# A recurrent trunk on one core: carried matrix memories in eight buffers instead of five, rotary tables loaded by the attention

## The chip, the core and the metric

The kernel runs on one core of a Trainium2 chip. The core has five engines that work side by side, each on its own list of instructions, in order: TensorE (PE in the profile) multiplies matrices, VectorE (DVE) and ScalarE (ACT) work on elements, GpSimd (POOL) does a few fills here, SyncE (SP) only issues DMAs. An instruction that waits holds up all that stands behind it on its engine. The metric is the device time of one execution in microseconds (us), as the median of several runs.

## What is computed

Two layers. Each normalises its input (512 prompt tokens and 8 samples of 16 tokens, 640 in all, 1024 wide), projects it with one large matrix, and feeds three mixers: a gated linear recurrence (RG-LRU), a matrix-memory recurrence (mLSTM, 4 heads of 256) and a sliding-window attention with rotary positions. Their outputs are projected, gated, added and projected again; an MLP with 4096 hidden channels follows. The part that matters here is the mLSTM's step with a carried memory C, which each of the 8 samples brings along for each head as a 256 x 256 matrix:

```python
def mlstm_chunk(carry, inp):
    C, n, m = carry
    q, k, v, ig, lf = inp
    ...
    num = jnp.einsum('bhts,bhsd->bhtd', w, v) + inter_w[..., None] * jnp.einsum('bhtd,bhde->bhte', q, C)
    ...
    C_new = decay[..., None, None] * C + jnp.einsum('bhs,bhsd,bhse->bhde', wk, k, v)
    n_new = decay[..., None] * n + jnp.einsum('bhs,bhsd->bhd', wk, k)
```

C is read, used against the queries of the 16 tokens, decayed, updated, and written out. In the attention, queries and keys are turned by cosines and sines of their positions (`rope`).

## The kernel before

All matmuls keep fp32 accuracy by splitting operands into a high and a low part (`split`, and for weights lines 164 and 166: ACT casts `wraw` to `whi`, DVE subtracts to get `wlo`), so that a product takes three matmuls. Weights stream from HBM through SP's queue (`wraw`, L212 and L155). The order of the instructions on each engine isn't written out by hand: a scheduler walks a simulated timeline when the kernel is built and takes on each engine what is ready, so work of different stages interleaves. Tiles come from pools; `bufs` is the number of buffers behind one name, and a new tile in a used buffer waits until all earlier work on that buffer is done.

`mlstm` runs over 4 heads. In each head four projections of the head's columns go through PE (L327): keys `ktok` (evicted by ACT), queries `qT` (DVE, L642), values `vt` (ACT, L649) and an output gate `mo`. The prompt's recurrence over chunks comes next, and in its last chunk `sample` (L577 to L624) handles the 8 samples. For each sample b:

- a buffer `cb` of 128 x 2 x 258 is taken (L600, five buffers), SP loads the sample's 256 KB matrix into it (L601), and DVE copies the two columns of the normaliser beside it (L602);
- ACT casts `cb` to `ch` (L605) and DVE makes the rest `cl` (L606), two buffers each;
- PE multiplies the queries `qm` with `ch` and `cl` (L609, four matmuls), and the stored rows `kvs` with one another (L613, two);
- DVE decays `cb` and adds the second product (L615, two instructions), SP stores `cb` to `out_C_s` (L617), and ACT takes the normaliser column (L618, `nsr`).

The rows in `kvs` go out to DRAM and come back in another layout (`sdr`, stores L585 and L586, loads L593), also on SP. Per layer that is 32 loads and 32 stores of 256 KB. The head ends with `num` (L731), scaled by DVE and transposed by PE (L737). The last lines of `mlstm` (L743 to L752) write the normalisers through a tile `nrt`.

The rotary tables `cos2` and `sin2` are columns 392 to 1031 of a constant tile `cs`, loaded at the start (L446) and kept in SBUF throughout. In each layer's `attention`, DVE multiplies them with a row of weights (L759 and L760). The sample part of it loads `vc` (L910), the old values of the window, and copies it (L912).

Of the kernel before, what the change touches and what calls it, by code (L numbers as in the profile page):

```python
# [9 lines left out]
F32 = mybir.dt.float32  # L10
# [45 lines left out]
NCST = 128 * 3 + 8 + 640  # L56
# [19 lines left out]
def trunk(ctx: ExitStack, tc: tile.TileContext, I, O):  # L76
    nc = tc.nc
    depth = I["w_in"].shape[0]
    cst = I["const"]
    pe, act, dve, pool, sp = nc.tensor, nc.scalar, nc.vector, nc.gpsimd, nc.sync  # L80

    const = ctx.enter_context(tc.tile_pool(name="const", bufs=1))
# [4 lines left out]
    psB = ctx.enter_context(tc.tile_pool(name="psB", bufs=4, space=PSUM))  # L87
    dram = ctx.enter_context(tc.tile_pool(name="scr", bufs=1, space=bass.MemoryType.DRAM))

    cs = const.tile([128, NCST], F32, name="cs")  # L90
    sp.dma_start(cs[:, 0:128], cst[:, 0:128])
    ident = cs[:, 0:128]
    maskp = cs[:, 128:256]
    masks = cs[:, 256:384]
    bmask = cs[:, 384:392]
    cos2 = cs[:, 392:712].rearrange("p (t d) -> p t d", d=64)
    sin2 = cs[:, 712:1032].rearrange("p (t d) -> p t d", d=64)
    ones = const.tile([128, 128], F32, name="ones")
    pool.memset(ones, 1.0)

# [8 lines left out]
    def ps_small():  # L109
        return psB.tile([128, 512], F32, name="psb", tag="psb")  # L110
# [16 lines left out]
    def split(dst, src, scale=None):  # L127

        if scale is None:
            act.copy(dst[:, 0], src)  # L130
            dve.tensor_tensor(dst[:, 1], src, dst[:, 0].bitcast(F32), ALU.subtract)
        else:
            act.activation(dst[:, 0], src, AF.Copy, scale=scale)  # L133
            dve.scalar_tensor_tensor(dst[:, 1], src, scale, dst[:, 0].bitcast(F32), op0=ALU.mult, op1=ALU.subtract)

    def act_tile(p=None):
        return (p or actp).tile([128, 2, NT], F32R, name="at", tag="at")
# [290 lines left out]
    with tc.tile_pool(name="ld", bufs=1) as ld:  # L428
        xin = ld.tile([128, 5, D], F32, name="xin")
        xss = ld.tile([128, 10], F32, name="xss")  # L430
        xpr = I["x_prompt"][0].rearrange("(t p) d -> p t d", p=128)

        def load(h):
            c = slice(512 * h, 512 * h + 512)
            sp.dma_start(xin[:, 0:2, c], xpr[:, 0:2, c])
            sp.dma_start(xin[:, 2:4, c], xpr[:, 2:4, c])
            sp.dma_start(xin[:, 4, c], I["x_sample"].rearrange("b s d -> (b s) d")[:, c])

        load(0)
        for _ in prep(0, 0):  # L440
            pass
        load(1)
        for _ in prep(0, 1):
            pass
        prepared[0] = 1
        sp.dma_start(cs[:, 128:NCST], cst[:, 128:NCST])  # L446
        xs, u = [], []
        for m in range(8):
            x = xp.tile([128, NT], F32, name="x", tag="x")
            ps = ps_small()  # L450
            for t in range(4):
                pe.transpose(ps[:, 128 * t:128 * t + 128], xin[:, t, 128 * m:128 * m + 128], ident)
            dve.tensor_copy(x[:, 0:512], ps)
            ps = ps_small()
            pe.transpose(ps[:, 0:128], xin[:, 4, 128 * m:128 * m + 128], ident)
            act.copy(x[:, 512:640], ps[:, 0:128])
            xs.append(x)
            u.append(act_tile())
            split(u[m], x, cv[:, 8 * V_N1 + m:8 * V_N1 + m + 1])
            if m % 4 == 1:  # L460
                h = m // 4
                for t in range(5):
                    xsq = ld.tile([128, 512], F32, name="xsq", tag="xsq", bufs=2)
                    act.activation(xsq, xin[:, t, 512 * h:512 * h + 512], AF.Square, accum_out=xss[:, 5 * h + t:5 * h + t + 1])
        dve.tensor_tensor(vv[:, 0:5], xss[:, 0:5], xss[:, 5:10], ALU.add)
# [86 lines left out]
    def mlstm(l, gp, gpp, mp, half, hdp):  # L552
# [24 lines left out]
        def sample(h, kw, vt, pn, out):  # L577


            st = mp.tile([128, 1028], F32R, name="st", tag="st", bufs=1)  # L580
            for o, n, src in ((0, 256, kw), (512, 258, vt[:, 4, :])):
                act.copy(st[:, o:o + n], src)
                dve.tensor_tensor(st[:, o + n:o + 2 * n], src, st[:, o:o + n].bitcast(F32), ALU.subtract)
            for i, (a, b) in enumerate(((0, 512), (0, 770), (256, 512))):
                sp.dma_start(sdr[h][:, i, 0:256], st[:, a:a + 256].bitcast(F32))  # L585
                sp.dma_start(sdr[h][:, i, 256:514], st[:, b:b + 258].bitcast(F32))  # L586

            def rows(g):

                kv = kvs[g % 2]  # L590
                sd = sdr[h][32 * g:32 * g + 32].rearrange("(b s) i d -> s i b d", s=16)
                for i in range(3):
                    sp.dma_start(kv[16 * i:16 * i + 16].bitcast(F32), sd[:, i])  # L593
                return kv

            pg = [ps_small(), ps_small()]
            for b in range(DB):
                if b % 2 == 0:
                    kv = rows(b // 2)
                cb = mp.tile([128, 2, 258], F32, name="cb", tag="cb", bufs=5)  # L600
                sp.dma_start(cb[:, :, 0:256], I["state_mlstm_C"][l, b, h].rearrange("(k p) e -> p k e", p=128))  # L601
                dve.tensor_copy(cb[:, :, 256:258], nT[:, :, 8 * b + 2 * h:8 * b + 2 * h + 2])  # L602
                ch = mp.tile([128, 2, 258], F32R, name="ch", tag="ch", bufs=2)
                cl = mp.tile([128, 2, 258], F32R, name="cl", tag="cl", bufs=2)
                act.copy(ch, cb)  # L605
                dve.tensor_tensor(cl, cb, ch.bitcast(F32), ALU.subtract)  # L606
                for kt in range(2):
                    for c in (ch, cl):
                        pe.matmul(pg[b // 4][:, 0:258], qm[:, kt, 128 * b:128 * b + 128], c[:, kt, :],  # L609
                                  start=(b % 4 == 0 and kt == 0 and c is ch), stop=(b % 4 == 3 and kt == 1 and c is cl))  # L610
                for kt in range(2):
                    ps = ps_small()
                    pe.matmul(ps[:, 0:258], kv[:, b % 2, 128 * kt:128 * kt + 128], kv[:, b % 2, 256:514],  # L613
                              start=True, stop=True)
                    dve.scalar_tensor_tensor(cb[:, kt, :], cb[:, kt, :], decb[:, h, 4 + b:5 + b], ps[:, 0:258],  # L615
                                             op0=ALU.mult, op1=ALU.add)
                sp.dma_start(O["C_s"][l, b, h].rearrange("(k p) e -> p k e", p=128), cb[:, :, 0:256])  # L617
                act.copy(nsr[:, b, h, :], cb[:, :, 256])  # L618
                if b % 4 == 3:

                    g = b // 4
                    here, there = slice(64 * g, 64 * g + 64), slice(64 - 64 * g, 128 - 64 * g)
                    act.copy(out[here], pg[g][there, 0:258])
                    dve.tensor_tensor(out[here], out[here], pg[g][here, 0:258], ALU.add)  # L624

        for h in range(4):
# [45 lines left out]
            for kt in range(2):  # L672
                dve.tensor_tensor(qs[:, kt, :], qT[:, kt, 128:512], iw[:, 0:384], ALU.mult)
                dve.tensor_tensor(qw[:, kt, :], qT[:, kt, 512:640], iw[:, 384:512], ALU.mult)
                d = qm[:, kt, :].rearrange("p (b t) -> p b t", t=144)
# [9 lines left out]
            for t in range(5):  # L685
# [30 lines left out]
                sq = mp.tile([128, 256], F32, name="sq", tag="sq", bufs=1)  # L716
# [15 lines left out]
            for e in range(2):  # L732
# [7 lines left out]
                pe.transpose(ps[:, 0:128], num[:, 4, 128 * e:128 * e + 128], ident)  # L740
                act.activation(yt[:, 512:640], ps[:, 0:128], AF.Copy, scale=half(V_MG, k))
                act.dma_start(ydr[0][128 * k:128 * k + 128, :], yt)
        nrt = mp.tile([8, 128], F32, name="nrt", tag="nrt")  # L743
        ps = ps_small()
        pe.transpose(ps[0:8, 0:128], npr, ident)
        dve.tensor_copy(nrt[0:8, :], ps[0:8, 0:128])
        sp.dma_start(O["n_p"][l, 0].rearrange("h (k p) -> (h k) p", p=128), nrt[0:8, :])
        nrs = mp.tile([64, 128], F32, name="nrs", tag="nrt")
        ps = ps_small()
        pe.transpose(ps[0:64, 0:128], nsr.rearrange("p b h k -> p (b h k)"), ident)  # L750
        dve.tensor_copy(nrs, ps[0:64, 0:128])
# [1 line left out]


    def attention(l, ap):
        def tables(o):
            tabs = ap.tile([128, 2, 5, 64], F32, name="tabs", tag="tabs")
            gq = rowb[:, o:o + 64].unsqueeze(1).to_broadcast([128, 5, 64])
            dve.tensor_tensor(tabs[:, 0], cos2, gq, ALU.mult)  # L759
            dve.tensor_tensor(tabs[:, 1], sin2, gq, ALU.mult)  # L760
            return tabs
# [37 lines left out]
        gemm_x(u, ev_kv)  # L799
        kd = ap.tile([128, 5, 2, 2, 64], F32, name="kd", tag="q", bufs=2)  # L800
        norm_rope(ksb[:, :, 0:128].rearrange("p t (h d) -> p t h d", d=64), 2, tables(64), kd[:, :, :, 0, :])
        act.copy(kd[:, :, :, 1, :], kd[:, :, :, 0, :])
        for nm, t_ in (("k", kd), ("v", vd)):
# [18 lines left out]
        qsm = ap.tile([128, 8, 8, 16], F32, name="qsm")  # L822
        pool.memset(qsm, 0.0)
        qtabs = tables(0)


# [173 lines left out]
    for l in range(depth):  # L1000
# [224 lines left out]
        with tc.tile_pool(name="at", bufs=1, reuse_waits="tile") as ap:  # L1225
            attention(l, ap)
# [18 lines left out]
        with tc.tile_pool(name="ml", bufs=1, reuse_waits="tile") as mp:  # L1245
            mlstm(l, gp, gpp, mp, half, hdp)
# [255 lines left out]
```

## Time and profile before

| | |
|---|---|
| median of 3 runs | 2889.65 us (2889.05, 2889.65, 2895.65) |
| profiled execution | 2888.68 us, its span 2886.9 us |
| PE busy | 2834.2 us, 98% |
| DVE busy | 1842.2 us, 64% |
| ACT busy | 1306.7 us, 45% |
| granted TensorE clock | 0.998 |

A busy share of 98% means that PE has 52.7 us of the span in which it stands still. The profile names for each such stretch the last event that released the engine. The mLSTM stages lie at about 480 to 840 us (layer 0) and 1930 to 2270 us (layer 1).

### The profile page before, as it was taken

The numbers are of one execution on the slowest core, as the hardware profiler recorded it, in microseconds if no ns is written. First come the engines' busy times: TensorE is split into PE (matmuls) and PEld (weight loads), VectorE is DVE, ScalarE is ACT, GpSimd is POOL, SyncE is SP. The second block draws the span as 40 slices with busy tenths as digits, with TensorE's granted clock in tenths as the row PEclk, the third lists the DMA queues.
The fourth block names the chain that finished last, engine by engine and source line by source line (L and its number), as shares of the span: only waits on it lengthen the run. The fifth ranks groups of instructions, "written<-read, shape, count | busy, mean of one in ns | idle before, by whom it ended". The sixth has DMA issues, their size and how long they took to land. (4 is left out here: it accounts for less than half of the span.)

```text
span 2886.9 us, 50824 instructions
## 1 busy us (share of the span) xinstructions
PE 2834.2 (98%) x20158; PEld 2794.1 (97%) x20158; DVE 1842.2 (64%) x3746; ACT 1306.7 (45%) x2761; POOL 26.7 (1%) x65
## 2 busy tenths in 40 slices
PE   8999999999999999999999999999999999999999
PEld 8999999999999999999999999999999999999999
DVE  7967576444554677676779676655455646767772
ACT  5764444333432444445357544443444424443452
POOL 0000000000000000000000000000000000000000
PEclk9999999999999999999999999999999999999999
DMA  5242224344474322222322322334444733222222
GB/s 174 65 124 81 71 86 124 117 134 143 150 259 132 110 75 87 81 74 87 113 61 79 117 72 86 94 101 142 127 142 148 268 121 103 74 88 74 81 81 81
DMA packets 276878, 319.53 MB, mean 111 GB/s; under 512 B 26424, under 2 KB 231016, under 8 KB 276608
## 3 DMA queue, kind: packets, MB, share of 16 engines
q1 hardware_dynamic: 267104, 300.03, 33.9%
q10 hardware_dynamic: 9536, 16.26, 1.6%
q8 instruction: 158, 2.59, 0.4%
q14 instruction: 80, 0.66, 0.1%
HBM read 255.76 MB, written 62.04 MB: 110 GB/s over the span
## 5 line engine op out<-in xcount | busy, mean ns | idle before, releaser
L309 PE MATMUL acc<-at,whi 128*128 128x320 f32 x5120 | 818.1, 312 | 6.8 <-ACT at L133 2.8
L309 PEld LDWEIGHTS acc<-at,whi 128*128 128x128 f32 x5120 | 765.3, 189 | 10.1 <-ACT at L133 3.5
L164 ACT CAST whi<-wraw 128x512 fp32r<-128x512 f32 x682 | 407.8, 619 | 489.0 <-PE acc L309 181.9
L166 DVE TENSOR_TENSOR wlo<-wraw,whi 128x512 fp32r<-128x512 f32 x682 | 451.4, 691 | 169.6 <-ACT whi L164 107.4
L327 PE MATMUL acc<-whi,at 128*128 128x256 f32 (+1 forms) x3040 | 408.3, 284 | 16.5 <-DVE qT L642 4.3
L309 PE MATMUL acc<-at,wlo 128*128 128x320 f32 x2560 | 415.0, 310 | 0.0
L327 PEld LDWEIGHTS acc<-whi,at 128*128 128x128 f32 x3040 | 377.9, 188 | 21.8 <-DVE qT L642 5.6
L309 PEld LDWEIGHTS acc<-at,wlo 128*128 128x128 f32 x2560 | 383.7, 188 | 0.7
L255 PE MATMUL acc<-at,whi 128*128 128x320 f32 x1440 | 245.0, 311 | 2.1 <-DVE ha L1375 0.6
L255 PEld LDWEIGHTS acc<-at,whi 128*128 128x128 f32 x1440 | 217.5, 188 | 8.3 <-ACT whi L164 4.7
L327 PE MATMUL acc<-wlo,at 128*128 128x256 f32 (+1 forms) x1520 | 218.0, 282 | 0.0
L327 PEld LDWEIGHTS acc<-wlo,at 128*128 128x128 f32 x1520 | 196.1, 188 | 0.2
L293 PE MATMUL psb<-at,whi 128*128 128x320 f32 x896 | 170.6, 309 | 0.0
L293 PE MATMUL acc<-at,whi 128*128 128x320 f32 x896 | 169.0, 309 | 0.0
L293 PEld LDWEIGHTS psb<-at,whi 128*128 128x128 f32 x896 | 141.3, 188 | 0.0
L293 PEld LDWEIGHTS acc<-at,whi 128*128 128x128 f32 x896 | 140.9, 188 | 0.0
L255 PE MATMUL acc<-at,wlo 128*128 128x320 f32 x720 | 133.5, 308 | 0.0
L164 ACT CAST whi<-wsum 128x512 fp32r<-128x512 f32 x120 | 74.2, 620 | 130.1 <-PE acc L293 100.1
L255 PEld LDWEIGHTS acc<-at,wlo 128*128 128x128 f32 x720 | 112.5, 188 | 0.0
L166 DVE TENSOR_TENSOR wlo<-wsum,whi 128x512 fp32r<-128x512 f32 x120 | 82.4, 687 | 44.8 <-ACT whi L164 39.1
L293 PE MATMUL acc<-at,wlo 128*128 128x320 f32 x448 | 101.7, 308 | 0.0
L293 PE MATMUL psb<-at,wlo 128*128 128x320 f32 x448 | 100.5, 308 | 0.0
(378 smaller groups left out, 3651.4 us busy)
## 6 DMA issues: line engine op xcount, KB each, us to landing
wraw<-in_w_in SPq DMA_DIRECT2D x160, 512.0 KB
wraw<-in_w_up SPq DMA_DIRECT2D x64, 512.0 KB
wraw<-in_w_down SPq DMA_DIRECT2D x64, 512.0 KB
cb<-in_state_mlstm_C SPq DMA_DIRECT2D x64, 256.0 KB
out_C_s<-cb SPq DMA_DIRECT2D x64, 256.0 KB
gdr<-sg ACTq DMA_DIRECT2D x32, 320.0 KB
rl<-ydr SPq DMA_DIRECT2D x32, 320.0 KB
sg<-gdr SPq DMA_DIRECT2D x32, 320.0 KB
```

The lines of the kernel that those rows point to most:

```text
L164: act.copy(hi if shape else hi[:, :, :src.shape[-1]], src)
L166: dve.tensor_tensor(lo if shape else lo[:, :, :src.shape[-1]], src, h.bitcast(F32), ALU.subtract)
L255: pe.matmul(bank[nm], ws[i][:, k, :], xs(nm, k)[:, part], start=(first and i == 0 and k == 0 and part == 0), stop=(i == 1 and k == 3), ski ...
L293: pe.matmul(o[s], lhs, hs[k][:, part, 320 * s:320 * s + 320], start=(k == 0 and i == 0 and part == 0), stop=(i == 1 and k == 3))
L309: pe.matmul(acc[:, s, 0:320], lhs, xs[k][:, part, 320 * s:320 * s + 320], start=(i == 0 and k == 0 and part == 0), stop=(i == 1 and k == 7),)
L327: pe.matmul(o, xs[k][:, part, 128 * t:128 * t + 128], wt[:, k % KQ, 0:n], start=(i == 0 and k == 0 and part == 0), stop=(i == 1 and k == 7),)
```

## The change

The tile `cs` shrinks from 1032 to 392 columns, which frees 2560 bytes in each partition; its load at the start shrinks with it. The rotary tables get a tile `trig` in the pool of each layer's attention, with a DMA of 320 KB of their own, once per layer. The buffers of `cb` go from five to eight, and the two tiles `nrt` and `nrs` share the buffer of `sq`.

```diff
--- before.py
+++ after.py
@@ -87,14 +87,12 @@
     psB = ctx.enter_context(tc.tile_pool(name="psB", bufs=4, space=PSUM))
     dram = ctx.enter_context(tc.tile_pool(name="scr", bufs=1, space=bass.MemoryType.DRAM))
 
-    cs = const.tile([128, NCST], F32, name="cs")
+    cs = const.tile([128, 392], F32, name="cs")
     sp.dma_start(cs[:, 0:128], cst[:, 0:128])
     ident = cs[:, 0:128]
     maskp = cs[:, 128:256]
     masks = cs[:, 256:384]
     bmask = cs[:, 384:392]
-    cos2 = cs[:, 392:712].rearrange("p (t d) -> p t d", d=64)
-    sin2 = cs[:, 712:1032].rearrange("p (t d) -> p t d", d=64)
     ones = const.tile([128, 128], F32, name="ones")
     pool.memset(ones, 1.0)
 
@@ -443,7 +441,7 @@
         for _ in prep(0, 1):
             pass
         prepared[0] = 1
-        sp.dma_start(cs[:, 128:NCST], cst[:, 128:NCST])
+        sp.dma_start(cs[:, 128:392], cst[:, 128:392])
         xs, u = [], []
         for m in range(8):
             x = xp.tile([128, NT], F32, name="x", tag="x")
@@ -597,7 +595,7 @@
             for b in range(DB):
                 if b % 2 == 0:
                     kv = rows(b // 2)
-                cb = mp.tile([128, 2, 258], F32, name="cb", tag="cb", bufs=5)
+                cb = mp.tile([128, 2, 258], F32, name="cb", tag="cb", bufs=8)
                 sp.dma_start(cb[:, :, 0:256], I["state_mlstm_C"][l, b, h].rearrange("(k p) e -> p k e", p=128))
                 dve.tensor_copy(cb[:, :, 256:258], nT[:, :, 8 * b + 2 * h:8 * b + 2 * h + 2])
                 ch = mp.tile([128, 2, 258], F32R, name="ch", tag="ch", bufs=2)
@@ -740,12 +738,12 @@
                 pe.transpose(ps[:, 0:128], num[:, 4, 128 * e:128 * e + 128], ident)
                 act.activation(yt[:, 512:640], ps[:, 0:128], AF.Copy, scale=half(V_MG, k))
                 act.dma_start(ydr[0][128 * k:128 * k + 128, :], yt)
-        nrt = mp.tile([8, 128], F32, name="nrt", tag="nrt")
+        nrt = mp.tile([8, 128], F32, name="nrt", tag="sq")
         ps = ps_small()
         pe.transpose(ps[0:8, 0:128], npr, ident)
         dve.tensor_copy(nrt[0:8, :], ps[0:8, 0:128])
         sp.dma_start(O["n_p"][l, 0].rearrange("h (k p) -> (h k) p", p=128), nrt[0:8, :])
-        nrs = mp.tile([64, 128], F32, name="nrs", tag="nrt")
+        nrs = mp.tile([64, 128], F32, name="nrs", tag="sq")
         ps = ps_small()
         pe.transpose(ps[0:64, 0:128], nsr.rearrange("p b h k -> p (b h k)"), ident)
         dve.tensor_copy(nrs, ps[0:64, 0:128])
@@ -753,6 +751,10 @@
 
 
     def attention(l, ap):
+        trig = ap.tile([128, 640], F32, name="trig")
+        sp.dma_start(trig, cst[:, 392:NCST])
+        cos2, sin2 = [trig[:, 320 * i:320 * i + 320].rearrange("p (t d) -> p t d", d=64) for i in range(2)]
+
         def tables(o):
             tabs = ap.tile([128, 2, 5, 64], F32, name="tabs", tag="tabs")
             gq = rowb[:, o:o + 64].unsqueeze(1).to_broadcast([128, 5, 64])
```

Lines of the changed kernel stand two lower than before up to `attention`, and two higher behind its new lines. What the scheduler makes of it is shown at three places. The first is SP's list where the first head's mLSTM begins (`dmat` and `iw` are rows of gates, `wraw` weights). Before:

```order
L670 DMA iw<-adr 128x512
L601 DMA cb<-in_state_mlstm_C 128x2x256 x3
L212 DMA wraw<-in_w_in 128x4x256
L601 DMA cb<-in_state_mlstm_C 128x2x256 x2
L212 DMA wraw<-in_w_in 128x4x256
L670 DMA iw<-adr 128x512
L212 DMA wraw<-in_w_in 128x4x256
L586 DMA sdr_80<-st 128x258 x2
L212 DMA wraw<-in_w_in 128x4x256
```

After:

```order
L668 DMA iw<-adr 128x512
L599 DMA cb<-in_state_mlstm_C 128x2x256 x3
L210 DMA wraw<-in_w_in 128x4x256
L599 DMA cb<-in_state_mlstm_C 128x2x256 x5
L210 DMA wraw<-in_w_in 128x4x256
L668 DMA iw<-adr 128x512
L210 DMA wraw<-in_w_in 128x4x256
L584 DMA sdr_80<-st 128x258 x2
L210 DMA wraw<-in_w_in 128x4x256
```

Five loads of `cb` have become eight. The second place is SP's list in the same head's loop over the samples, from the fifth store (`out_C_s`) on. Before:

```order
L617 DMA out_C_s<-cb 128x2x256
L601 DMA cb<-in_state_mlstm_C 128x2x256
L617 DMA out_C_s<-cb 128x2x256
L601 DMA cb<-in_state_mlstm_C 128x2x256
L212 DMA wraw<-in_w_in 128x4x256
L617 DMA out_C_s<-cb 128x2x256
L212 DMA wraw<-in_w_in 128x4x256
L601 DMA cb<-in_state_mlstm_C 128x2x256
L617 DMA out_C_s<-cb 128x2x256
L670 DMA iw<-adr 128x512
L601 DMA cb<-in_state_mlstm_C 128x2x256
L212 DMA wraw<-in_w_in 128x4x256 x2
```

After:

```order
L615 DMA out_C_s<-cb 128x2x256
L599 DMA cb<-in_state_mlstm_C 128x2x256
L615 DMA out_C_s<-cb 128x2x256
L599 DMA cb<-in_state_mlstm_C 128x2x256
L210 DMA wraw<-in_w_in 128x4x256 x2
L615 DMA out_C_s<-cb 128x2x256 x2
L668 DMA iw<-adr 128x512
L599 DMA cb<-in_state_mlstm_C 128x2x256 x2
L210 DMA wraw<-in_w_in 128x4x256
```

The loads stand at nearly the same places between the stores (two now together behind the last store), but with three more resident from the start each of them fetches a matrix three further on: behind a head's first store it is the first matrix of the next head. The third is DVE's list where the first attention begins (`sinkp`, `stmp` and `sinks` are small rows of it). Before:

```order
L768 TENSOR_TENSOR stmp<-rowb,cs 128x16
L759 TENSOR_TENSOR tabs<-cs,rowb 128x320
L760 TENSOR_TENSOR tabs<-cs,rowb 128x320
L770 TENSOR_REDUCE sinks<-stmp 128x2
L912 COPY vc<-vc 128x8x64
L166 TENSOR_TENSOR wlo<-wraw,whi 128x2x256 x2
L166 TENSOR_TENSOR wlo<-wraw,whi 128x528 x2
L780 TENSOR_REDUCE nsm<-t_2294 128x10
L781 TENSOR_SCALAR nsm<-nsm 128x10
```

After:

```order
L767 COPY sinkp<-rowb 64x8
L770 TENSOR_TENSOR stmp<-rowb,cs 128x16
L772 TENSOR_REDUCE sinks<-stmp 128x2
L761 TENSOR_TENSOR tabs<-trig,rowb 128x320
L762 TENSOR_TENSOR tabs<-trig,rowb 128x320
L914 COPY vc<-vc 128x8x64
L164 TENSOR_TENSOR wlo<-wraw,whi 128x2x256 x2
L164 TENSOR_TENSOR wlo<-wraw,whi 128x528 x2
L782 TENSOR_REDUCE nsm<-t_2296 128x10
L783 TENSOR_SCALAR nsm<-nsm 128x10
```

The two products of the tables now read `trig`, and `sinks` has moved ahead of them. On SP the load of `trig` stands directly ahead of the one of `vc`.

## Rows read from the trace of the kernel before

**Rows 1.** The page: the span, and its part 1, busy time of each engine.

```profile
span 2886.9 us, 50824 instructions
...
PE 2834.2 (98%) x20158; PEld 2794.1 (97%) x20158; DVE 1842.2 (64%) x3746; ACT 1306.7 (45%) x2761; POOL 26.7 (1%) x65
```

**Rows 2.** PE's waits over the span: waiting line, releaser: us in total, times, longest.

```profile
PE psb L609 <- ACT ch L605: 5.5, 6, 1.3
PE acc L327 <- DVE qT L642: 4.3, 4, 1.4
...
PE acc L327 <- ACT vt L649: 3.5, 7, 0.6
...
PE psb L737 <- DVE num L731: 2.7, 2, 1.5
...
PE psb L613 <- DVE cb L615: 2.3, 4, 1.1
...
PE psb L613 <- issue: 1.0, 2, 0.6
...
PE psb L609 <- DVE cl L606: 0.7, 2, 0.3
```

**Rows 3.** Timeline of PE: start us, us, engine, line, operation, count, idle before.

```profile
548.53 0.29 PE L609 MATMUL psb<-cl,qm 128*128 128x258 f32 x1
548.65 0.28 PE L609 MATMUL psb<-ch,qm 128*128 128x258 f32 x1
```

**Rows 4.** Timeline of PE: the four waits for ch behind a load.

```profile
570.16 0.39 PE L609 MATMUL psb<-ch,qm 128*128 128x258 f32 x1 [1.34 <-ACT ch L605]
...
734.13 0.39 PE L609 MATMUL psb<-ch,qm 128*128 128x258 f32 x1 [1.18 <-ACT ch L605]
...
2005.31 0.39 PE L609 MATMUL psb<-ch,qm 128*128 128x258 f32 x1 [1.06 <-ACT ch L605]
...
2253.27 0.39 PE L609 MATMUL psb<-ch,qm 128*128 128x258 f32 x1 [0.56 <-ACT ch L605]
```

**Rows 5.** Timeline of ACT: copies into ch that waited for a load.

```profile
569.48 0.62 ACT L605 CAST ch<-cb 128x516 fp32r<-128x516 f32 x1 [5.64 <-DMA cb<-in_state_mlstm_C]
...
655.84 0.62 ACT L605 CAST ch<-cb 128x516 fp32r<-128x516 f32 x1 [1.80 <-DMA cb<-in_state_mlstm_C]
...
2179.94 0.62 ACT L605 CAST ch<-cb 128x516 fp32r<-128x516 f32 x1 [2.76 <-DMA cb<-in_state_mlstm_C]
```

**Rows 6.** Timeline of PE: pauses for qT and vt, first and last of five.

```profile
658.32 1.92 PE L327 MATMUL acc<-whi,at 128*128 128x256 f32 x14 [1.03 <-DVE qT L642]
...
2181.08 2.15 PE L327 MATMUL acc<-whi,at 128*128 128x256 f32 x16 [0.61 <-ACT vt L649]
```

**Rows 7.** The tile cb: what its engines waited for, us and times.

```profile
  DMA cb<-in_state_mlstm_C: 50.9, 21
...
  DMA out_C_s<-cb: 33.4, 19
```

**Rows 8.** Windows: stretch, length, busy us of PE, PEld, DVE, ACT, POOL; PEclk, DMA share, GB/s.

```profile
10.00:20.00 10.00, 9.12 (x57) 8.20 (x56) 9.69 (x18) 10.00 (x28) 0.00 (x0) 1.00 1.05 394
505.00:510.00 5.00, 5.00 (x45) 5.00 (x44) 0.31 (x2) 1.10 (x3) 0.00 (x0) 1.00 0.02 5
```

**Rows 9.** Timeline of SP: a store issued, and the load that waited for it.

```profile
562.10 0.42 SPq L617 DMA_DIRECT2D out_C_s<-cb  x1
...
566.48 1.34 SPq L601 DMA_DIRECT2D cb<-in_state_mlstm_C  x2
```

**Rows 10.** Timelines of SP, DVE and PE in the first attention.

```profile
180.02 0.58 SPq L910 DMA_DIRECT2D vc<-in_cache_v  x1
...
188.84 0.43 DVE L912 COPY vc<-vc 128x512 f32<-128x512 f32 x1 [5.57 <-DMA vc<-in_cache_v]
190.41 2.53 DVE L166 TENSOR_TENSOR wlo<-wraw,whi 128x512 fp32r<-128x512 f32 x4 [1.14 <-ACT whi L164]
...
195.56 2.50 PE L309 MATMUL acc<-at,wlo 128*128 128x320 f32 x16
```

## Prediction

> **What bounds the kernel now.** The page's busy times come first: TensorE (PE) works 2834.2 of the 2886.9 us of the span, 98% [rows 1]. The kernel computes matmuls from end to end, the change removes none, and so only the 52.7 us in which PE stands still can be won. The list of PE's waits says which of them lie where the change works: the seven lines of it that belong to the mLSTM stages (two stages, one per layer) hold 27 pauses and 5.5 + 4.3 + 3.5 + 2.7 + 2.3 + 1.0 + 0.7 = 20.0 us [rows 2]. The other 32.7 us lie in stages whose code stays as it is.
>
> A pause costs somewhat more than the list says, since the record of the last matmul before it lasts longer than its share: such a matmul is recorded with 0.28 us, but the next one starts 0.12 us later [rows 3]. So each pause hides about 0.16 us more, and the ceiling is 20.0 + 27 x 0.16 = 24.3 us, 0.8% of the time.
>
> Then one asks each pause what it came from. Four waits of PE for `ch` add up to 1.34 + 1.18 + 1.06 + 0.56 = 4.14 us [rows 4]. At the first, ACT's copy into `ch` had itself stood 5.64 us until its load of `cb` landed [rows 5]; the other three are alike. Five more pauses stand behind such a load without showing it: ACT and DVE execute in order, and where ACT waits for `cb`, the eviction of `vt` (ACT) or `qT` (DVE, behind `cl`, which needs `ch`) comes late. At 655.84 ACT had waited 1.80 us for a load, and 658.32 is a pause for `qT`; at 2179.94 it had waited 2.76 us, and 2181.08 is one for `vt` [rows 5, 6]. These five (two for `qT`, three for `vt`; the first and the last are shown) hold 3.4 us. Over the whole kernel ACT waits 21 times and 50.9 us for loads of `cb` [rows 7]; most of it PE never feels.
>
> The remaining 18 pauses have other causes. In ten (four for `cb`, two for `cl`, two issue, and the two waits for `ch` that no load explains: 2.3 + 0.7 + 1.0 + 1.4 = 5.4 us) DVE is late, mostly because its copy of L602 into a buffer waits until the store of the buffer's last content has landed: 19 such waits, 33.4 us [rows 7]. The other eight (two `qT`, four `vt`, two `num`: 2.5 + 1.8 + 2.7 = 7.0 us) come from the order in which DVE and ACT take their work.
>
> **The change part by part.** *Eight buffers.* The order shows it: three loads more are issued at the start of the stage, a whole head is resident, and where SP loaded batch 5 of the same head after the first store, it now loads batch 0 of the next head. Before, a load could go out only 3.0 us ahead of its use: the one issued at 566.48 [rows 9] let ACT begin at 569.48 [rows 5]. Now eight batches lie between the two instead of five. The three extra loads at the stage's start cost nothing: DMA moves 5 GB/s in 505 to 510 us [rows 8]. The load-bound pauses go: 4.14 + 4 x 0.16 = **-4.8 us** (0 to -4.8). The five behind them: 3.4 + 5 x 0.16 = 4.2 us, of which I take **-3.2** (0 to -4.2), since `qT` and `vt` still stand in queues with other work. The eight of order are 7.0 + 8 x 0.16 = 8.3 us; the scheduler writes DVE's, ACT's and PE's order anew, and some of them move away: **-2.5** (0 to -8.3).
>
> The ten pauses that come from stores stay: **0** (0 to -(5.4 + 10 x 0.16) = -7.0). The copy of L602 still waits for the store of its buffer's last content, and it still stands in DVE's order just behind it. SP too: the store issued at 562.10 lets the next load go at 566.48, 4.4 us later [rows 9], and behind that load wait SP's next store and the `kvs` loads. More buffers don't shorten that distance, for the scheduler puts the next load right after the store that frees its buffer, however far ahead its use lies.
>
> (The Trainium skill, "DMA: Bandwidth & Descriptors", section "Latency and other measured facts", says that a DMA's fixed cost of about 2 us is mainly the round trip to the target memory, and slowest into HBM. That speaks against this change: by it the store's landing, not the load, is the wait that lasts, and the -4.8 and -3.2 could come back as waits for stores, which is the first rival below. Here the distance is 4.4 us, so the trace agrees that a store is slow to land.)
>
> The new order brings waits of its own. None is visible in it; the nearest row is the old order's store pauses, 7.0 us, so 0 to +7.0, and I take **+2.0**, nearer to zero, because the pieces in the two orders are largely the same.
>
> *Tables out of the constants.* The first load shrinks by 320 KB, which at the 394 GB/s of 10 to 20 us [rows 8] is 0.8 us of a phase in which DMA is full: **-0.3** (0 to -0.8). Each attention now loads 320 KB on SP, and DVE's two tables wait for it. No row of before shows it; the nearest is `vc`, the next load on SP, for which DVE stood 5.57 us [rows 10]. The tables come before the `vc` copy on DVE, so if both land together nothing moves. Behind them stand the weight parts `wlo`, four in 2.53 us from 190.41 on, the first of them thus by 191.1; PE takes them from 195.56 on [rows 10], 4.4 us later. **0**, by that cover. Were the two loads to land one behind the other, with `vc` 8.8 us later than now (its own time from issue to DVE's copy, 180.02 to 188.84), it would be (8.8 - 4.4) x 2 = +8.8.
>
> *Buffer `nrt` under another tag:* 0; the second copy waited for the first one's store before, and still does.
>
> Sum: -4.8 - 3.2 - 2.5 + 2.0 - 0.3 = -8.8 us. The profiled execution took 2888.68 us, so 2879.9; the median of the runs, 2889.65, lies 1.0 above it, so **2880.9 us**.
>
> **Rivals.** *Stores take the place of loads* (25%). `ch` is early, but `cl` needs DVE, which stands in L602 for a store's landing; the four pauses return as waits for `cl`, the two of `qT` stay, and new order costs what it wins. What remains is the three pauses of `vt`, 1.7 + 3 x 0.16 = 2.1 us: 2888.68 - 2.1 + 1.0 = 2887.6. For it speaks that DVE's waits for stores, 33.4 us, are two thirds of ACT's for loads [rows 7], against it that at the four pauses ACT was the late one.
>
> *Nearly every pause goes* (11%). All 17.3 us of the three groups and half of the stores' 7.0: -20.8, that is 2868.9. A new order could do it, but it has no reason to move all. (The Trainium skill, "Perfetto Trace Analysis", section "Optimization Strategy", says that the same gap, repeated on the engine that should be full, can mean too few buffers. By it this would be the outcome; the trace bears it out for 9 of the 27 pauses.)
>
> *DVE's stalls multiply* (7%), slower than before. 48 of the 64 copies of L602 use a buffer that was stored before. 19 waits cost PE at most 7.0 us now, 0.37 each; if all 48 wait, 48 x 0.37 = 17.7, that is +10.7, and with `cl` behind them the gains above don't come: 2888.68 + 10.7 + 1.0 = 2900.4. It decides from some 40 waits on. Against it: the copies stand at nearly the same places of DVE's order as before.
>
> *The tables' load in series with `vc`* (3%): +8.8 eats the gain, 2889.7.
>
> **How the numbers follow.** Forecast 54%, rivals 25, 11, 7 and 3%. About 0.3%, 8.7 us, is what a measurement of this kernel can tell from no change; faster by that is below 2881.0. My forecast lies on that edge, so I give 30 of its 54 to faster and 24 to the same. Faster: 30 + 11 = 41%. Same: 24 + 25 + 3 = 52%. Slower: 7%. The range takes in the forecast with its bounds, the stores' rival, the tables' and most of the second: 2868 to 2892; the 7% and some tails are left out.
>
> **What the profile after would show.** ACT's waits for loads of `cb` fall from 50.9 us to under 15; PE's for `ch` from 5.5 to under 2, with `vt` and `qT` at about half; DVE's for `out_C_s` stay at 25 to 40 us. PE's idle time in the two stages falls from 20.0 to some 13 us. If DVE's waits for stores grow and `cl` and `cb` take `ch`'s place in PE's list, the first or third rival is right. If the tables' line waits over 4 us longer than `vc` did and PE waits for `wlo` after it, the last is. The forecast is wrong in its main step if ACT's waits for loads vanish and PE's idle time doesn't move.

## The result, and the profile after

The changed kernel takes 2871.37 us (median of 5 runs, 2869.63 to 2874.25) against 2890.48 us (5 runs, 2889.05 to 2895.65): a ratio of 0.9932, 95% interval 0.992 to 0.9944, 19.1 us less. The forecast was 2880.9 us within 2868 to 2892: the sign was right and the time lies in the range, but the gain is a little over twice the forecast, and faster had got 41% there, the same 52%.

The page after, beside [rows 1]:

```profile
span 2869.0 us, 50842 instructions
...
PE 2829.2 (99%) x20158; PEld 2793.1 (97%) x20158; DVE 1841.9 (64%) x3746; ACT 1310.8 (46%) x2761; POOL 26.8 (1%) x65
```

The span is 17.9 us shorter. PE stands still for 2869.0 - 2829.2 = 39.8 us instead of 52.7, 12.9 less; the other 5.0 us are PE time that was booked as busy, and by the count of matmuls nearly all of it lies in the two stages. The same matmuls are issued. Where the idle time went is read from PE's waits in the two stages, layer 0 first; columns as in [rows 2]:

```profile
PE psb L735 <- DVE num L729: 0.9, 1, 0.9
PE psb L611 <- issue: 0.9, 1, 0.9
PE acc L325 <- DVE qT L640: 0.8, 1, 0.8
PE acc L325 <- ACT vt L647: 0.5, 1, 0.5
PE psb L611 <- DVE den L713: 0.2, 1, 0.2
...
PE psb L735 <- DVE num L729: 0.9, 1, 0.9
PE acc L325 <- DVE qT L640: 0.9, 1, 0.9
PE acc L325 <- ACT vt L647: 0.5, 1, 0.5
PE psb L611 <- issue: 0.4, 1, 0.4
PE psb L607 <- DVE cl L604: 0.3, 1, 0.3
PE psb L611 <- DMA kvs<-sdr: 0.3, 1, 0.3
PE psb L611 <- DVE cb L613: 0.2, 1, 0.2
```

Twelve pauses of 6.8 us are left of the 27 of 20.0 us [rows 2]. None is a wait for `ch` any more. What the tile `cb` was waited for, beside [rows 7]:

```profile
  DVE cb L613: 53.7, 37
  DMA out_C_s<-cb: 39.2, 24
  PE psb L607: 25.4, 16
  PE psb L611: 19.9, 10
  DMA wraw<-in_w_in: 8.1, 2
  ACT ch L603: 6.7, 11
  ACT whi L162: 0.4, 1
```

The line for loads, 50.9 us in 21 waits before, is gone. The one for stores has grown from 33.4 us (19) to 39.2 (24). The timeline of DVE at the first attention shows the tables, beside [rows 10]:

```profile
189.12 0.49 DVE L761 TENSOR_TENSOR tabs<-trig,rowb 128x320 f32<-128x320 f32 x1 [6.25 <-DMA trig<-in_const]
189.53 0.48 DVE L762 TENSOR_TENSOR tabs<-trig,rowb 128x320 f32<-128x320 f32 x1
189.93 0.42 DVE L914 COPY vc<-vc 128x512 f32<-128x512 f32 x1
190.47 2.53 DVE L164 TENSOR_TENSOR wlo<-wraw,whi 128x512 fp32r<-128x512 f32 x4
```

DVE waits 6.25 us for the tables instead of 5.57 for `vc`, which then has landed too; the weight parts begin at 190.47 instead of 190.41, and nothing of it reaches PE.

### The profile page after: what moved, and what is told of

Read it like the earlier page. It is cut to its first block, busy times and chain, and to the rows that moved or that the text cites. A ratio compares the mean times of both kernels' runs of the same rounds, so it can differ in the third digit from the quotient of the medians.

```text
span 2869.0 us, 50842 instructions
## 1 busy us (share of the span) xinstructions
PE 2829.2 (99%) x20158; PEld 2793.1 (97%) x20158; DVE 1841.9 (64%) x3746; ACT 1310.8 (46%) x2761; POOL 26.8 (1%) x65
## 4 chain that ended last, share of the span: by engine, by line
PE 91%; ACT 3%; DVE 2%; DMA 2%; issue 1%; SPq 0%; DVEq 0%; ACTq 0%
PE acc L307 36%; PE acc L325 17%; PE acc L253 11%; PE acc L291 7%; PE psb L291 7%; PE psb L253 2%; PE psb L895 2%; DMA out_C_s<-cb 1%; PE psb L865 1%; PE acc L272 1%; PE psb L700 1%; PE psb L1166 1%; PE psb L887 1%; PE psb L607 1%; ACT whi L162 1%
```

## Experiments

Each run was timed beside the kernel before on its chip; a ratio is to that, with its 95% interval. The first theory is that of the forecast: loads of `cb` that come late stop ACT, which works in order, and through ACT and DVE stop PE. The rivals are that DVE's waits for stores cost the time, and that the scheduler merely happened on a better order. A run's waits and pauses are read from one execution, its time from all of them.

**Tables only, and the dose of buffers.** The edit is one number in the changed kernel:

```diff
-                cb = mp.tile([128, 2, 258], F32, name="cb", tag="cb", bufs=8)
+                cb = mp.tile([128, 2, 258], F32, name="cb", tag="cb", bufs=5)
```

and 6 and 7 in the second and third.

> The changed kernel with five buffers for the carried matrices, so only the tables (own tile, loaded twice) and the shared buffer of nrt are left of the change. If the gain of 19 us comes from the buffers, this lies within 2 us of the kernel before (2888 to 2892), with ACT's waits for loads of cb near 50 us again. If the smaller first load or a new order of instructions that came with the tables brought it, it lies clearly below 2885.

> The changed kernel with six buffers. If the time follows the loads that come too late, one buffer more takes a part of ACT's waits for loads of cb (50.9 us before, none after), say to 20 to 30 us, and the time falls by a like share of the 19 us: 2878 to 2885. If the gain is an accident of the order that the scheduler happened on with eight, the time doesn't follow the waits: anywhere from 2870 to 2895.

> The changed kernel with seven buffers. By the theory of late loads ACT's waits for cb are nearly gone, under 15 us, and the time is 2871 to 2878, between that of six and that of eight. By the theory of an accident of the order it needn't lie between them.

| buffers | us | ratio | ACT's waits for loads | DVE's waits for stores |
|---|---|---|---|---|
| 5 (tables moved) | 2892.72 | 1.0002 (0.9993 to 1.0011) | 44.3 us, 21 | 34.1 us, 19 |
| 6 | 2874.19 | 0.9936 (0.9924 to 0.9949) | 6.8 us, 2 | 36.2 us, 28 |
| 7 | 2874.67 | 0.9937 (0.9925 to 0.995) | none | 45.5 us, 27 |
| 8 (the change) | 2871.37 | 0.9932 (0.992 to 0.9944) | none | 39.2 us, 24 |

The tables by themselves change nothing. The time follows ACT's waits and not DVE's; but nearly all of it, over 90% of the gain, comes with the sixth buffer. I had expected a share of it. "A whole head ahead" is more than is needed: in the tile `cb` of the kernel with six buffers two waits for loads are left.

```profile
  DMA out_C_s<-cb: 36.2, 28
...
  DMA cb<-in_state_mlstm_C: 6.8, 2
```

**DVE's waits for stores, taken away at five buffers.** Two ways. In the first the normaliser's columns no longer go through `cb`:

```diff
-                dve.tensor_copy(cb[:, :, 256:258], nT[:, :, 8 * b + 2 * h:8 * b + 2 * h + 2])
...
+                nc_ = nT[:, :, 8 * b + 2 * h:8 * b + 2 * h + 2]
...
-                act.copy(ch, cb)
+                act.copy(ch[:, :, 256:258], nc_)
+                act.copy(ch[:, :, 0:256], cb)
```

(likewise for `cl` and the update). In the second the copy of L602 goes to POOL: `pool.tensor_copy` for `dve.tensor_copy`.

> Five buffers, but the normaliser's two columns are no longer copied into cb: ACT and DVE take them from nT beside it (a small ACT copy and three small DVE instructions more per sample, one ACT copy and one DVE copy less), so that DVE has no instruction left that waits for a store to land. If late loads are the cause, ACT still waits for loads of cb, 40 to 60 us, and at most the ten pauses from stores go: 2882 to 2890. If DVE's waits for stores were what held PE, the 33 us of them go and most of the 19 us with them: 2870 to 2877.

> The same with five buffers: DVE waits for no store, but the loads are as late as before. By the theory of late loads at most the ten pauses ascribed to stores go, 7 us: 2884 to 2891, and ACT's waits for loads stay near 45 us. If DVE's waits for stores were the cause, it is 2870 to 2878.

They took 2898.78 us (1.0023, 1.0014 to 1.0032) and 2888.83 us (0.9997, 0.9988 to 1.0005). DVE waits for no store in either, and nothing is gained; ACT's waits for loads are 48.7 us (23) and 67.4 us (26). So it isn't enough at five buffers to take DVE's waits away. Neither run shows that they cost nothing, for each edit brought costs of its own: in the second PE's six waits for `ch` grew from 5.5 to 8.9 us, while of the eight under `cb`, `cl` and issue (4.0 us before) one of 0.8 us is left. The first is 8.8 us over the upper end that I gave it: it has 128 more DVE instructions, and a lower clock, told below.

**Late loads with eight buffers.** This holds the number of buffers and makes only the loads late. `issue_after` puts the load behind a named store in SP's order, without a wait for its landing:

```diff
+        stores = []
...
-                sp.dma_start(cb[:, :, 0:256], I["state_mlstm_C"][l, b, h].rearrange("(k p) e -> p k e", p=128))
+                with tc.issue_after(stores[-4]) if len(stores) >= 4 else ExitStack():
+                    sp.dma_start(cb[:, :, 0:256], I["state_mlstm_C"][l, b, h].rearrange("(k p) e -> p k e", p=128))
...
+                stores.append(sp.dma_start(O["C_s"][l, b, h].rearrange("(k p) e -> p k e", p=128), cb[:, :, 0:256]).ins)
```

and with 5, 6 and 7 in place of 4.

> The changed kernel with its eight buffers, but each load of cb stands on SP behind the store of the sample four before it (in order only, it doesn't wait until that store has landed). So the loads go out about as late as with five buffers, while no copy of L602 meets a fresh store. If late loads alone made the 19 us, they come back: ACT waits 40 us and more for loads of cb, PE's pauses in the two stages are near 20 us, and the time is 2885 to 2895. If the buffers worked otherwise (through DVE's waits for stores, or through SP's), it stays under 2878.

> The same with the sample five before: a load goes out right behind the store whose landing SP waited for with five buffers, some 3.5 us sooner than there. A load then has 6 to 7 us where it took 3. By the theory of late loads ACT's waits for cb fall under 15 us and the time is 2870 to 2878: the landing of the store on SP, not the fifth buffer as such, was what made them late. By the rival, that a whole head must lie ahead, it is 2880 and more.

Late by four: 2899.53 us, ratio 1.0032 (1.002 to 1.0045), slower than the kernel before although it has eight buffers and DVE waits for no store at all. Its tile `cb`:

```profile
  DMA cb<-in_state_mlstm_C: 58.1, 35
```

PE's pauses in its stage of layer 0:

```profile
PE acc L325 <- ACT vt L650: 5.0, 2, 3.9
PE acc L325 <- DVE qT L643: 1.4, 1, 1.4
PE psb L610 <- ACT ch L606: 1.3, 2, 1.0
PE psb L614 <- DVE csum L625: 1.3, 1, 1.3
PE acc L307 <- ACT ktok L638: 0.6, 1, 0.6
PE psb L614 <- DMA kvs<-sdr: 0.4, 1, 0.4
```

With layer 1 there are 15 of 17.6 us, near the 20.0 that I had expected; the time is 4.5 us over my range, and part of that is the clock, told below. One place shows the chain in full, ACT first, then PE:

```profile
660.27 0.62 ACT L606 CAST ch<-cb 128x516 fp32r<-128x516 f32 x1 [2.26 <-DMA cb<-in_state_mlstm_C]
660.79 0.19 ACT L619 COPY nsr<-cb 128x2 f32<-128x2 f32 x1
662.51 0.19 ACT L619 COPY nsr<-cb 128x2 f32<-128x2 f32 x1 [1.53 <-DVE cb L616]
662.61 0.83 ACT L650 ACTIVATE vt<-acc,rtok 128x256 f32<-128x256 f32 x2
...
663.13 3.40 PE L325 MATMUL acc<-whi,at 128*128 128x256 f32 x16 [3.88 <-ACT vt L650]
```

A load is late and `ch` waits; with it DVE's update of that `cb` is late, for which ACT stands another 1.53 us in `nsr`. The two evictions of `vt` stand behind both on ACT, and PE waits 3.88 us for a buffer of its accumulator. PE's list names `vt`; the cause is the load.

Late by five: 2863.75 us, ratio 0.9911 (0.9896 to 0.9926). The difference between the two is one sample's distance, with the same buffers and no wait of DVE for a store in either, and it is 36 us: late loads are shown as a cause. But it is also 7.6 us faster than the changed kernel, which I had not expected, since its loads are not early. In layer 0, loads stand less than 5 us ahead of `ch` 16 times in 32 before, never in the changed kernel, and 12 times here (counted from the timelines of SP and ACT). ACT still waits, but shortly, 15.0 us in 12 waits:

```profile
  DVE cb L616: 37.4, 29
  PE psb L610: 29.9, 20
  PE psb L614: 26.2, 14
  ACT ch L606: 20.8, 27
  DMA cb<-in_state_mlstm_C: 15.0, 12
  ACT nsr L619: 0.8, 2
```

There is no line for `out_C_s` any more. In the stage of layer 0 PE has no pause, and in that of layer 1 it has two:

```profile
PE acc L307 <- ACT ktok L638: 0.6, 1, 0.6
PE psb L614 <- DMA kvs<-sdr: 0.5, 1, 0.5
```

**What the changed kernel still pays.** Two waits are gone in that run: DVE's for the landing of stores (39.2 us in the changed kernel) and SP's, here before and after the change:

```profile
SPq L601 <- DMA out_C_s<-cb: 111.0, 52, 5.3
...
SPq L599 <- DMA out_C_s<-cb: 89.0, 46, 4.9
```

To tell them apart, the copy of L602 went to POOL with eight buffers, so that only SP waits for stores; then, since POOL's queue also holds the memsets of `vt`, once more with these on DVE.

> The changed kernel with the copy of L602 (the normaliser's columns into cb) on POOL instead of DVE, so that POOL and not DVE waits for stores to land (39 us of DVE's waits). If these waits still cost PE something, the 12 pauses left in the stages (6.7 us) shrink and the time falls by 2 to 6 us, to 2865 to 2869. If DVE has the time to spare, it is the same within 2 us. The memsets of vt stand behind the copies on POOL and could hold PE: then it is longer.

> As the run with eight buffers and the copy of L602 on POOL, with the two memsets of vt taken from POOL to DVE, so that nothing PE needs stands behind POOL's waits for stores. SP still waits for the stores' landing as in the changed kernel, DVE waits for none. If DVE's waits for stores are what the changed kernel still pays against the kernel whose loads are late by five samples (2863.75 us), this comes out at 2862 to 2867; if SP's waits are, at 2869 to 2873.

2871.45 us (0.9932, 0.9919 to 0.9944) and 2869.94 us (0.9927, 0.9915 to 0.9939): no different from the changed kernel. In the first a new wait of 4.6 us came up, the only large one of its stage:

```profile
PE acc L325 <- ACT mo L630: 4.6, 1, 4.6
```

From the other side, the loads were moved on step by step with eight buffers:

> Eight buffers, each load behind the store of the sample six before it. Loads go out one sample sooner than with five, and the buffer they take was stored two samples before. If what counts is that a load has some 3 us more than it needs and that no store is waited for that was just issued, this is as good as five or a little better: 2860 to 2865. If waits for stores' landing come back, it moves towards the changed kernel: 2866 to 2872.

> Eight buffers, each load behind the store of the sample seven before it, so that the buffer it takes was stored just one sample before. Loads have time enough (ACT should wait under 2 us for them). If what the changed kernel still pays are waits for stores that were just issued, they come back here in part: DVE waits 20 to 35 us for out_C_s, and the time is 2866 to 2871, between the run late by six (2864.5) and the changed kernel (2871.4). If early loads are all that counts, it is 2862 to 2865.

| loads | us | ratio | ACT for loads | DVE for stores | SP's loads for stores | PE's pauses in the stages |
|---|---|---|---|---|---|---|
| late by 4 | 2899.53 | 1.0032 | 58.1 us, 35 | none | none | 17.6 us, 15 |
| late by 5 | 2863.75 | 0.9911 | 15.0 us, 12 | none | none | 1.1 us, 2 |
| late by 6 | 2864.47 | 0.9908 (0.9895 to 0.9922) | 1.2 us, 1 | 14.3 us, 9 | none | 1.7 us, 3 |
| late by 7 | 2865.76 | 0.9914 (0.9901 to 0.9928) | none | 27.2 us, 22 | 10.5 us, 9 | 2.7 us, 5 |
| the change | 2871.37 | 0.9932 | none | 39.2 us, 24 | 89.0 us, 46 | 6.8 us, 12 |
| the change, copy on POOL, `vt` on DVE | 2869.94 | 0.9927 | none | none | 108.8 us, 43 | 4.8 us, 7 |

("None" for SP: no such line among SP's waits.) The time moves little while DVE's waits go from nothing to 27 us ("late by 7" came out just under the range that I had given to waits for stores), and little when they are taken from 39 to nothing with SP's left. Read so, it goes with SP's. But the last row is no clean test. 2.7 of its 4.8 us are pauses for `mo`, which the changed kernel doesn't have: at the longer one, 2.15 us, ACT had waited 6.67 us for another tile ahead of `mo` (7.71 us at the 4.6 us shown above), and behind it the granted clock was 0.57 for 4 us, 1.7 us of PE time. Without these 4.4 us the run would come out at some 2865.5, an estimate, beside the three late ones. Each of these edits also moves the order of work on PE, DVE and ACT, the intervals of the change and of "late by" 5, 6 and 7 overlap at their ends, and no run took SP's waits away alone. That late loads had to go is shown; how the last 6 to 8 us divide between SP's waits, DVE's and the order stays open.

That the scheduler merely happened on a better order is unlikely over all runs: seven different orders in which ACT waits at most 6.8 us for loads, and the one with 15.0 us in short waits, lie at 2863.75 to 2874.67 us, those with 22.3 us and more at 2881.70 to 2899.53.

**Six buffers in that order.** "Late by 5" with `bufs=6`, to see whether the two spare buffers are needed:

> Six buffers, each load behind the store of the sample five before it: the same places for the loads as in the best run, but the buffer a load takes was stored only one sample before. If that store has mostly landed, 2863 to 2868, and two buffers (4 KB per partition) less are needed. If SP and DVE wait for it, as with six buffers without that order, 2870 to 2876.

2881.70 us (0.9972, 0.9961 to 0.9982), worse than both: slower than six buffers without the order (2874.19) too. Its tile `cb`:

```profile
  DMA out_C_s<-cb: 27.7, 24
  DMA cb<-in_state_mlstm_C: 22.3, 8
```

SP's loads wait for stores only 9.7 us here, yet ACT waits 22.3 us for loads in 8 waits, 2.8 each, against 6.8 us without the order and 1.25 each in the best run. Again the time follows ACT's waits for loads, above all long ones; why they are late in this order stays open. So of eight buffers without an order and six the times hardly differ (0.9932 and 0.9936), and only the order makes use of the other two. By the sizes six should have had place beside the tables: three buffers take 3 x 2064 = 6192 bytes of a partition, of which the tables gave 2560 and `nrt` 512, so 3120 had been free before. No run tried that.

## Why the prediction was right, and which of its terms were off

- *What bounds it.* Right: 12.9 of the 17.9 us of the span are PE's idle time, all of it in the two stages (20.0 to 6.8 us; outside of them it grew by 0.3).
- *What a pause hides.* Too small. 15 pauses fewer took 5.0 us of booked busy time with them, 0.33 us each, where I had read 0.16 from the pitch of the matmuls [rows 3]. The matmul behind a pause is recorded with 0.39 us [rows 4] against 0.28 in a row, 0.11 us of the difference; the rest I can't place. It isn't the clock, granted in full through both stages in both traces. This is 2.6 us of the error, and the ceiling was nearer to 20.0 + 27 x 0.33 = 28.9 than to 24.3.
- *Load-bound waits for `ch`, -4.8.* Right: all four went. *The five behind them, -3.2 of 4.2.* Right in kind, and I held back 1.0 without need.
- *The eight of order, -2.5.* About right: the two `num`, two `qT` and two `vt` that are left hold 4.5 us of their 7.0, 2.5 less, with two pauses fewer.
- *The ten from stores, 0.* Here the step failed. I had put them down to DVE's copy of L602, and DVE's waits did stay, as I said (33.4 to 39.2 us); but six pauses of 2.3 us are left of ten of 5.4, the two for `ch` gone. What made the other eight, 4.0 us under `cb`, `cl` and issue, stays open. Under these and like names (`den`, `csum`, `nsr`, `kvs` and others) PE stands 6.1 us in the run with the tables alone, 2.3 with early loads and DVE's waits kept (the change), and 0.5 late by five, with DVE's waits gone and loads late only by little. With late loads and DVE's waits gone it is 1.9 us late by four and 1.6 with the copy on POOL at five buffers, but 7.1 without the copy into `cb`, where DVE has more to do. So neither DVE's waits nor late loads account for them alone. These are single executions, each in an order of its own.
- *New waits of the new order, +2.0.* Nearly none came: two of the six just counted stand under names that PE didn't wait for before, `den` and `kvs`, 0.5 us together.
- *Tables, 0, and the first load, -0.3.* The tables cost nothing, as worked out: DVE waits for them where it waited for `vc`. Of the smaller first load nothing is seen; the run with the tables alone is at 1.0002.
- *Sum.* By the list -4.1 - 3.4 - 2.5 - 3.1, 13.1 us, and 15 x 0.33 = 5.0: 18.1 us, against 17.9 of the span. The outcome lies near the second rival ("nearly every pause goes", 2868.9), which I gave 11%.
- *Rivals.* That stores take the place of loads, and that DVE's stalls multiply, are out: DVE's waits did grow, but all that PE still stands still in the stages is 6.8 us. The Trainium skill ("DMA: Bandwidth & Descriptors", "Latency and other measured facts") puts a DMA's fixed cost mainly down to the round trip to the target memory, with HBM the slowest. The waits of SP for stores to land, up to 5.3 us before, agree that a store is slow to land. Its waits and DVE's are gone or shorter in the runs late by five to seven, which are another 6 to 8 us faster; which of the two counts stays open, as said. The tables in series with `vc` didn't happen: `vc` was copied at 189.93 without a wait.

## What to carry to other kernels

Ask a pause on the bound engine not only what released it, but what the releasing engine itself had waited for just before: here pauses under three names (`ch`, `qT`, `vt`) were one cause, a load that came late for an engine that works in order. Look at the distance between a store and the load that reuses its buffer: if the load's queue waits for a store that was only just issued, the load goes out late by that wait, 2.1 us on average and 5.3 at most here before (111.0 us in 52 waits). One buffer more lets loads go out further ahead of their use, though the queue still waits (99.7 us in 49 waits with six); an order that reuses an older buffer takes the wait itself away. Then try the smallest number that nearly ends the waits for loads, here six, and try an order of your own beside the scheduler's: eight buffers with the loads put five samples behind gave 2863.75 us, less than eight buffers alone (2871.37; the intervals overlap at their ends) and than the kernel before. The same order with six buffers was worse, 2881.70.

## What was not expected of the hardware

A pause can cost twice. In the run late by four, the 16 matmuls behind the pause of 3.88 us took 3.40 us; with a pause of 0.45 us before them the same 16 took 2.17 in the changed kernel:

```profile
659.68 2.17 PE L325 MATMUL acc<-whi,at 128*128 128x256 f32 x16 [0.45 <-ACT vt L647]
```

The windows of the late run show the granted clock (the column before the DMA share) right behind that pause:

```profile
658.00:663.00 5.00, 1.26 (x11) 1.05 (x9) 2.58 (x12) 1.21 (x6) 0.00 (x0) 1.00 0.51 162
663.00:666.00 3.00, 2.87 (x15) 2.87 (x16) 2.66 (x14) 0.44 (x2) 0.00 (x0) 0.60 0.61 175
666.00:669.00 3.00, 3.00 (x23) 3.00 (x23) 1.06 (x3) 1.08 (x3) 0.00 (x0) 0.83 0.00 0
```

PE was busy for 1.26 of 5 us, and then the clock averaged 0.60 and 0.83 of full over the next 6 us, that is, it stood in part at the lower level of 1.2 GHz: 3.0 x 0.40 + 3.0 x 0.17 = 1.7 us of PE time. The kernel before had pauses of 1.5 us at most in these stages, and its clock stayed up there in the profiled execution. But the length of a pause alone doesn't decide it. The same 1.37 us ahead of the same 16 matmuls, first in the kernel before, then in the run with the tables alone and its clock behind that pause:

```profile
579.31 2.15 PE L327 MATMUL acc<-whi,at 128*128 128x256 f32 x16 [1.37 <-DVE qT L642]
...
580.22 3.25 PE L325 MATMUL acc<-whi,at 128*128 128x256 f32 x16 [1.37 <-DVE qT L640]
...
581.00:584.00 3.00, 3.00 (x16) 3.00 (x16) 2.51 (x15) 0.49 (x2) 0.00 (x0) 0.50 0.93 264
```

In the kernel before the clock stayed at 1.00 there. The mean clock of two longer runs tells the same: 0.996 late by four and 0.995 without the copy into `cb`, against 0.998 before and after. 0.3% of 2890 us are 8.7 us, of the size of what the latter lost beyond what I had expected.
